# Six token blocks transposed beside the first attention, and four column tiles of their projection behind the first selection's products

## The chip, the cores and the metric

The kernel runs on one core of a Trainium2 chip. The metric is the device time of one execution in microseconds. The engines are named as the profile names them: PE does the matrix products and the transposes, PEld its weight loads, DVE is the vector engine, ACT the scalar engine, POOL the engine that also issues the indirect gathers, SP the queue that issues most other transfers. Each engine works through its own list of instructions in a fixed order.

## The reference

One decoder layer over 1024 tokens of width 1024, in float32:

```
x   = layer_norm(x)
mix = concat(fox_attention(x @ w_in), hgrn2(x @ w_in)) @ w_out
x   = layer_norm(alpha * x + mix)
q   = x @ w_q                            # 8 heads x 2 halves x 128
s   = q . sub_keys                       # 128 scores per half
top 16 of each half; top 16 of the 256 sums -> 128 experts e per token, gates g
h   = gelu(x . u_tab[e]) * g             # 128 numbers per token
y   = sum over e of h * v_tab[e]
out = layer_norm(alpha * x + y)
```

`fox_attention` has 8 causal heads of 64 with a forget bias, `hgrn2` 4 heads with a 128 x 128 state, worked through in chunks. There are 16,384 experts. Their part is computed in two ways: four of the eight blocks of 128 tokens fetch their experts' rows with gathers, the other four use a dense product with all experts, in which gates that were not chosen are zero.

## The kernel before

**Precision.** A float32 operand is split in a high and a low part (ACT copies to the high, DVE or POOL subtracts), and a product is three matrix products: high by high, low by high, high by low (`mm3`, L289 to L295). A weight block of 128 x 1024 so needs one load (`wraw`), one ACT copy (`whi`, L215) and one subtraction (`wlo`, L218). `transpose_split` (L267) turns a token block on PE and splits it out of PSUM (`xh` on ACT, `xl` on DVE at L286; with a third pool it goes by ACT's `tsx` copy at L283 and POOL at L284).

**Stages.** `mixers` (L323) takes the tokens as three groups of 256, 512 and 256. For each: the attention and the recurrence (`fox`, `hgrn`, interleaved), `mix_out` (the output projection, the residual, the norm, 16 transposes and their split `mh`, `ml`), `select` (scores, and DVE's top-16 searches) and `select_tail` (pair builds `oh`, `ij` on DVE, `sel`). The input projection is done twice: for the first group at the start, and for the later 768 tokens in one go behind the first group's `select_tail`. `preload` (L438) loads those six token blocks, `project` (L418) turns and splits them while the tail runs, and `project_cols` (L446) computes 17 column tiles (weights `wt`, 24 products 512 wide and 24 products 256 wide each) and then six groups of `wn` columns (144 products each).

**Side work.** The gathers and the one-hot matrices that the dense part needs are generators in three lists: `ujobs` (rows of `u`, one dot product each on DVE at L1124), `vjobs` (rows of `v`, accumulated on DVE at L1149 for three of the four blocks and on PE for one) and `bjobs` (the one-hots of the dense blocks, built on DVE at L962 and multiplied on PE). `tick` (L176) is called in every stage with the stage's name; it adds RATE times a weight to what is owed to each list, up to 16, and runs steps while something is owed. HOLD keeps the first list still for some ticks. What is left of the gathers runs in the dense part: `dense` (L1019) goes over 128 chunks of experts, products on PE, splits and sums (`dy`) on DVE, and a `tick` between. Gathered rows go through eight buffers named `rows`; `ys` is the accumulator of L1149, 128 x 1024 float32 in SBUF. `psy` is a PSUM pool with one tile `y` of two banks.

The order on each engine is set by the scheduler from the order of the code and the operations' priorities. The list above is the order of the code.

Of the kernel before, what the change touches and what calls it, by code (L numbers as in the profile page):

```python
# [8 lines left out]
F32 = mybir.dt.float32  # L9
F32R = mybir.dt.float32r  # L10
# [19 lines left out]
NROWS = 8  # L30
# [8 lines left out]
VDVE = (1, 6, 7)  # L39
HOLD = 7  # L40
# [7 lines left out]
GORD = (0, 1, 2, 3, 4, 5)  # L48
Q = {"qk": "a", "hs": "a"}
SEND0 = 0  # L50
# [22 lines left out]
class Layer:  # L73
    def __init__(self, ctx, tc, a, out, dbg=None):
        self.ctx, self.tc, self.nc, self.a, self.out = ctx, tc, tc.nc, a, out
        self.dbg = dbg
        self.nw, self.slabs = 0, 1
        self.ujobs, self.vjobs, self.bjobs, self.owed = [], [], [], [0.0] * 3
        self.nu = self.nv = 0
        self.hold = 0.0  # L80
# [94 lines left out]

    def tick(self, phase, T=None, w=1.0):  # L176
        rate = RATE[phase] if T is None else RATE[phase][T]
        self.hold = max(self.hold - w, 0.0)
# [144 lines left out]
    def mixers(self, groups, es):  # L323
        st, gb, tl = ExitStack(), ExitStack(), ExitStack()
        self.lx = ExitStack()
# [4 lines left out]
        for n, (t0, T) in enumerate(groups):  # L330
# [5 lines left out]
            if n < 2:  # L336
                tl.close()
            po = st.enter_context(self.pool("po", 1, "left"))
            whole = f"m{n}" in WHOLE
# [22 lines left out]
            pos = pz.tile([P, nq, 8, 16], U32, name="pos", tag="pos")  # L362
            if n == 0:
                x1 = self.preload(T, S - T)
            self.select(t0, T, mh, ml, sv, si, best, pos, T == 256 or EARLY)
# [9 lines left out]
            if n == 0:  # L375
                x1 = self.project(T, S - T, st, x1)
                self.lx.close()
            tail = self.select_tail(t0, T, sv, si, best, pos, T == 256 or EARLY, pw)
# [41 lines left out]
    def project(self, t0, T, st, xs=None):  # L420
        pa = st.enter_context(self.pool("pa", 1, "right"))
        xh = pa.tile([P, DC, T], F32R, name="xh", tag="xh")
        xl = pa.tile([P, DC, T], F32R, name="xl", tag="xl")

        def split(n, x):
            self.transpose_split("f", x, xh, xl, n)

        if t0:
            with self.pool("pt", 2, "right") as pt:
                for n, x in enumerate(xs):  # L430
                    self.transpose_split("f", x, xh, xl, n, pt if n % 2 < PSPL else None)
        else:
            pl = self.lx.enter_context(self.pool("pl", 2, "left"))
            self.first_ln(pl, 0, T, split)
            self.lns = [lambda r0=r0: self.first_ln(pl, r0, 2 * P, lambda n, x: None) for r0 in range(T, S, 2 * P)]
        return xh, xl

    def preload(self, t0, T):  # L438
        pl = self.lx.enter_context(self.pool("pl", 1, "left"))
        xs = []  # L440
        for n in range(T // P):
            x = pl.tile([P, D], F32, name="x", tag="x", bufs=T // P)
            self.q("x1l").dma_start(x, self.d_x1[t0 + n * P : t0 + (n + 1) * P])
            xs.append(x)
        return xs

    def project_cols(self, t0, T, xh, xl):
        nc, a = self.nc, self.a
        nq = T // P
        tsl = slice(t0, t0 + T)  # L450
        with self.pool("pb", 2, "right") as pb:
            for m in range(17):
                po = self.projT(self.weight(pb, a["wt"][m], "p1" if t0 else "p0"), xh, xl, T)
# [645 lines left out]

    def rows(self):  # L1100
        return self.gp.tile([P, D], F32, name="rows", tag="rows", bufs=NROWS)

# [26 lines left out]
    def gather_v(self, blk, u):  # L1129
# [6 lines left out]
        if blk in VDVE:  # L1136
            ys = gp.tile([P, D], F32, name="ys", tag="ys")
            ei = sel[:, 0].bitcast(I32)
# [178 lines left out]
```

## Time and profile before

| | |
|---|---|
| median of 3 runs | 3062.12 us (3060.14 to 3067.3) |
| the profiled execution | 3096.88 us, its span 3094.9 us |
| PE busy | 2628.0 us (85%), 15865 instructions |
| DVE busy | 2664.9 us (86%), 5563 instructions |
| POOL busy | 1614.0 us (52%), 1216 instructions |
| ACT busy | 1076.2 us (35%), 2004 instructions |
| HBM read, written | 821.67 MB, 62.42 MB |

The profiled execution stands 34.76 us above the median. In time the profile reads as follows: the first group's projection to about 121 us, its attention to 195, `mix_out` to 233, `select` to 298, `select_tail` to 352.5, the later tokens' projection to 584, the second group to about 1085, the third group's attention to 1343, its `mix_out` to 1366 and `select` with the rest of the one-hots to 1523, and the dense part from about 1595 to 3060. The row of PE's granted clock is between 0.7 and 0.9 up to the dense part and 0.9 and more in it.

### The profile page before, as it was taken

Reading aid. Unit: us, or ns where it says so; the run is one execution under the profiler, and the core shown is the slowest. Engines: PE = TensorE matmul, PEld = TensorE weight load, DVE = VectorE, ACT = ScalarE, POOL = GpSimd, SP = SyncE. Lnnn points to the kernel's source line nnn. Section 1 sums busy time; section 2 is a strip of 40 time slices with the busy share of each in tenths; the row PEclk is TensorE's granted clock in tenths of the full one; section 3 lists DMA queues with packets and bytes.
Section 4 is the critical chain, followed back from the end, with each engine's and each line's share of the span. In section 5 each row is a group of like instructions: output and inputs, shape, how many; then the busy total and the mean of one; then the engine's idle time right before and its main releaser. Section 6 shows DMA issues by size and latency. Waiting matters only on the chain. (4 is left out here: it accounts for less than half of the span.)

```text
span 3094.9 us, 45136 instructions
## 1 busy us (share of the span) xinstructions
PE 2628.0 (85%) x15865; PEld 2150.5 (69%) x15865; DVE 2664.9 (86%) x5563; ACT 1076.2 (35%) x2004; POOL 1614.0 (52%) x1216
## 2 busy tenths in 40 slices
PE   7767799777769767878469899999989999999995
PEld 6767689755557445667458778787768877877874
DVE  8658766588669986689888999999999999999998
ACT  4733222364222333476323223223223323222331
POOL 2344476565756644200045666665567665656652
PEclk9878899797889888889589999999999999999997
DMA  7542599754978856864479999999999999999994
GB/s 277 191 150 75 196 349 322 229 163 153 343 252 293 275 159 234 304 248 177 182 248 365 332 369 367 356 367 360 347 360 367 382 381 356 363 365 341 369 340 157
DMA packets 338659, 887.10 MB, mean 287 GB/s; under 512 B 29912, under 2 KB 124136, under 8 KB 336000
## 3 DMA queue, kind: packets, MB, share of 16 engines
q0 software_dynamic: 147456, 536.94, 47.5%
q1 hardware_dynamic: 185200, 338.38, 31.3%
q10 hardware_dynamic: 5776, 8.90, 0.8%
q8 instruction: 125, 2.05, 0.3%
q14 instruction: 102, 0.84, 0.1%
HBM read 821.67 MB, written 62.42 MB: 286 GB/s over the span
## 5 line engine op out<-in xcount | busy, mean ns | idle before, releaser
L1105 POOL DMA_INDIRECT rows<-in_u,gsel x512 | 687.4, 1343 | 617.8 <-DVE rows L1124 408.3
L1105 POOL DMA_INDIRECT rows<-in_v,gsel x512 | 642.8, 1256 | 444.5 <-DVE ys L1149 259.8
L1124 DVE SCALAR_TENSOR_TENSOR rows<-rows,gx 128x1024 f32<-128x1024 f32 x512 | 627.9, 1273 | 40.7 <-DMA rows<-in_u,gsel 20.5
L1149 DVE SCALAR_TENSOR_TENSOR ys<-rows,sd,ys 128x1024 f32<-128x1024 f32 x381 | 488.8, 1283 | 0.6
L293 PE MATMUL psh<-dxh,uh 128*128 128x512 f32 x1024 | 402.9, 393 | 29.4 <-ACT uh L1031 16.5
L295 PE MATMUL psh<-dxh,ul 128*128 128x512 f32 x1024 | 400.7, 391 | 9.5 <-DVE ul L1032 9.4
L294 PE MATMUL psh<-dxl,uh 128*128 128x512 f32 x1024 | 400.2, 391 | 0.0
L294 PE MATMUL psf<-vl,hh 128*128 128x512 f32 x768 | 309.9, 404 | 42.6 <-DVE vl L1032 41.8
L1031 ACT ACTIVATE vh<-vr 128x512 fp32r<-128x512 f32 x256 | 161.8, 632 | 429.2 <-PE psv L295 392.1
L295 PE MATMUL psf<-vh,hl 128*128 128x512 f32 x768 | 305.2, 397 | 0.0
L293 PE MATMUL psf<-vh,hh 128*128 128x512 f32 x768 | 278.8, 395 | 11.7 <-DVE dy L1064 8.1
L1031 ACT ACTIVATE uh<-ur 128x1024 fp32r<-128x1024 f32 x128 | 136.0, 1063 | 413.0 <-PE psh L294 386.2
L293 PEld LDWEIGHTS psh<-dxh,uh 128*128 128x128 f32 x1024 | 193.5, 189 | 77.2 <-ACT hs L1045 19.1
L295 PEld LDWEIGHTS psh<-dxh,ul 128*128 128x128 f32 x1024 | 193.5, 189 | 50.6 <-DVE ul L1032 10.5
L294 PEld LDWEIGHTS psh<-dxl,uh 128*128 128x128 f32 x1024 | 193.5, 189 | 39.5
L294 PEld LDWEIGHTS psf<-vl,hh 128*128 128x128 f32 x768 | 147.8, 192 | 89.6 <-DVE vl L1032 59.0
L215 ACT ACTIVATE whi<-wraw 128x1024 fp32r<-128x1024 f32 x106 | 111.5, 1056 | 231.5 <-issue 62.8
L1032 DVE TENSOR_TENSOR vl<-vr,vh 128x512 fp32r<-128x512 f32 x256 | 169.6, 683 | 13.9 <-ACT vh L1031 13.9
L293 PEld LDWEIGHTS psf<-vh,hh 128*128 128x128 f32 x768 | 145.1, 189 | 49.8 <-DVE dy L1064 9.6
L218 DVE TENSOR_TENSOR wlo<-wraw,whi 128x1024 fp32r<-128x1024 f32 x60 | 81.8, 1364 | 106.7 <-ACT whi L215 94.4
L295 PEld LDWEIGHTS psf<-vh,hl 128*128 128x128 f32 x768 | 147.9, 193 | 29.9
L1032 DVE TENSOR_TENSOR ul<-ur,uh 128x1024 fp32r<-128x1024 f32 x128 | 156.2, 1221 | 12.3 <-ACT uh L1031 11.2
(341 smaller groups left out, 6155.9 us busy)
## 6 DMA issues: line engine op xcount, KB each, us to landing
ur<-in_ut SPq DMA_DIRECT2D x128, 512.0 KB
vr<-in_v SPq DMA_DIRECT2D x256, 256.0 KB
d_g<-slab SPq DMA_DIRECT2D x16, 2048.0 KB
gt<-d_g SPq DMA_DIRECT2D x32, 1024.0 KB
wraw<-in_wq SPq DMA_DIRECT2D x48, 512.0 KB
wraw<-in_wt SPq DMA_DIRECT2D x34, 512.0 KB
wraw<-in_wn SPq DMA_DIRECT2D x24, 512.0 KB
wraw<-in_wo SPq DMA_DIRECT2D x24, 512.0 KB
```

What stands on the lines that cost most here:

```text
L215: nc.scalar.activation(hi, raw, AF.Copy)
L218: eng.tensor_tensor(lo, raw, hi.bitcast(F32), op=ALU.subtract)
L293: mm(out, lh, rh, start=start, stop=False, **kw)
L294: mm(out, lh, rl, start=False, stop=False, **kw)
L295: mm(out, ll, rh, start=False, stop=stop, **kw)
L1031: nc.scalar.activation(hi, raw, AF.Copy)
L1032: nc.vector.tensor_tensor(lo, raw, hi.bitcast(F32), op=ALU.subtract)
L1105: self.nc.gpsimd.indirect_dma_start(out=t, out_offset=None, in_=tab, in_offset=bass.IndirectOffsetOnAxis(ap=idx, axis=0))
L1124: self.pin(nc.vector.scalar_tensor_tensor(u, u, 1.0, x2, op0=ALU.mult, op1=ALU.mult, accum_out=sd[:, n : n + 1]), "u")
L1149: self.pin(nc.vector.scalar_tensor_tensor(ys, v, h, ys, op0=ALU.mult, op1=ALU.add), "w")
```

## The change

A generator `early` does what `preload` and `project` did for the six later token blocks, and the first four (NEARLY) of the 17 column tiles. `tick` advances it in the first group's attention (0.34 of a step for each tick there, some 18 ticks, so six steps) and returns without serving the three lists, or adding to what they are owed, while it lives (before, the first group's ticks left `bjobs` at its cap of 16 before it had a job; now it starts from nothing in the third group's attention); what is left, the four tiles, is emitted behind `select` and ahead of `select_tail`. The splits of the token blocks are on ACT and DVE, none on POOL; the four tiles' weights go through `rows` buffers, their low halves on DVE, their products into the PSUM tile `y`. HOLD goes from 7 to 3.5, and the accumulator at L1149 from SBUF to the PSUM tile `y`.

```
@@ -37,7 +37,7 @@
     "dense": (5.4, 5.4, 0),
 }
 VDVE = (1, 6, 7)
-HOLD = 7
+HOLD = 3.5
 LNM = (3, 6, 9)
 QB, PRB = {256: 2, 512: 2}, {2: 3, 4: 7}
 VRAW = 5
@@ -46,6 +46,8 @@
 FAST = {"x": 2, 0: 2, 256: 2, 768: 2}
 FLN = 9
 GORD = (0, 1, 2, 3, 4, 5)
+NEARLY = 4
+ERATE = {"fox": 0.34, "hgrn": 0.0, "mix": 0.0, "sel": 0.0}
 Q = {"qk": "a", "hs": "a"}
 SEND0 = 0
 WDIV = {"p0": 0, "m0": 1, "s0": 1, "p1": 3, "m1": 2, "s1": 2, "m2": 1, "s2": 1}
@@ -76,6 +78,7 @@
         self.dbg = dbg
         self.nw, self.slabs = 0, 1
         self.ujobs, self.vjobs, self.bjobs, self.owed = [], [], [], [0.0] * 3
+        self.ahead, self.due = None, 0.0
         self.nu = self.nv = 0
         self.hold = 0.0
         self.lnf = None
@@ -174,6 +177,12 @@
         yield
 
     def tick(self, phase, T=None, w=1.0):
+        if self.ahead and phase in ERATE:
+            self.due += w * ERATE[phase]
+            while self.due >= 1.0:
+                self.due -= 1.0
+                next(self.ahead, None)
+            return
         rate = RATE[phase] if T is None else RATE[phase][T]
         self.hold = max(self.hold - w, 0.0)
         for n, q in enumerate((self.ujobs, self.vjobs, self.bjobs)):
@@ -321,7 +330,7 @@
         return po
 
     def mixers(self, groups, es):
-        st, gb, tl = ExitStack(), ExitStack(), ExitStack()
+        st, gb, tl, ex = ExitStack(), ExitStack(), ExitStack(), ExitStack()
         self.lx = ExitStack()
         init = self.setup()
         next(init)
@@ -335,6 +344,11 @@
             st.close()
             if n < 2:
                 tl.close()
+            ex.close()
+            if n == 0:
+                pa = ex.enter_context(self.pool("pa", 1, "right"))
+                x1 = [pa.tile([P, DC, S - T], F32R, name=m, tag=m) for m in ("xh", "xl")]
+                self.ahead = self.early(T, S - T, *x1, pa)
             po = st.enter_context(self.pool("po", 1, "left"))
             whole = f"m{n}" in WHOLE
             mh = po.tile([P, DC, T], F32 if whole else F32R, name="mh", tag="mh")
@@ -360,8 +374,6 @@
             si = pz.tile([P, nq, 16, 16], U32, name="si", tag="si")
             best = pz.tile([P, nq, 8, 16], F32, name="best", tag="best")
             pos = pz.tile([P, nq, 8, 16], U32, name="pos", tag="pos")
-            if n == 0:
-                x1 = self.preload(T, S - T)
             self.select(t0, T, mh, ml, sv, si, best, pos, T == 256 or EARLY)
             if late:
                 self.drain(self.bjobs)
@@ -373,8 +385,8 @@
                 dense = self.dense_prep(es)
             pw = tl.enter_context(self.pool("pw", 1, "right"))
             if n == 0:
-                x1 = self.project(T, S - T, st, x1)
-                self.lx.close()
+                self.drain([self.ahead])
+                self.ahead = None
             tail = self.select_tail(t0, T, sv, si, best, pos, T == 256 or EARLY, pw)
             if T == 256:
                 tail = self.tail_gather(t0, T, tail)
@@ -425,31 +437,49 @@
         def split(n, x):
             self.transpose_split("f", x, xh, xl, n)
 
-        if t0:
-            with self.pool("pt", 2, "right") as pt:
-                for n, x in enumerate(xs):
-                    self.transpose_split("f", x, xh, xl, n, pt if n % 2 < PSPL else None)
-        else:
-            pl = self.lx.enter_context(self.pool("pl", 2, "left"))
-            self.first_ln(pl, 0, T, split)
-            self.lns = [lambda r0=r0: self.first_ln(pl, r0, 2 * P, lambda n, x: None) for r0 in range(T, S, 2 * P)]
+        pl = self.lx.enter_context(self.pool("pl", 2, "left"))
+        self.first_ln(pl, 0, T, split)
+        self.lns = [lambda r0=r0: self.first_ln(pl, r0, 2 * P, lambda n, x: None) for r0 in range(T, S, 2 * P)]
         return xh, xl
 
-    def preload(self, t0, T):
-        pl = self.lx.enter_context(self.pool("pl", 1, "left"))
-        xs = []
+    def early(self, t0, T, xh, xl, pa):
+        nc, a = self.nc, self.a
         for n in range(T // P):
-            x = pl.tile([P, D], F32, name="x", tag="x", bufs=T // P)
+            x = self.rows()
             self.q("x1l").dma_start(x, self.d_x1[t0 + n * P : t0 + (n + 1) * P])
-            xs.append(x)
-        return xs
+            pt = self.psy.tile([P, D], F32, name="y", tag="y")
+            for c in range(DC):
+                nc.tensor.transpose(pt[:, c * P : (c + 1) * P], x[:, c * P : (c + 1) * P], self.ident)
+            sl = slice(n * P, (n + 1) * P)
+            for c0 in range(0, DC, 4):
+                v = pt[:, c0 * P : (c0 + 4) * P].rearrange("p (c t) -> p c t", c=4)
+                h = xh[:, c0 : c0 + 4, sl]
+                nc.scalar.activation(h, v, AF.Copy)
+                nc.vector.tensor_tensor(xl[:, c0 : c0 + 4, sl], v, h.bitcast(F32), op=ALU.subtract)
+            yield
+        for m in range(NEARLY):
+            raw, hi, lo = self.rows(), self.rows(F32R), self.rows(F32R)
+            self.q("w").dma_start(raw, a["wt"][m])
+            nc.scalar.activation(hi, raw, AF.Copy)
+            nc.vector.tensor_tensor(lo, raw, hi.bitcast(F32), op=ALU.subtract)
+            wh, wl = (t.rearrange("p (c m) -> p c m", c=DC) for t in (hi, lo))
+            po = self.psy.tile([P, D], F32, name="y", tag="y")
+            s = pa.tile([P, T], F32, name="es", tag="es", bufs=2)
+            for c0 in range(0, T, 512):
+                cs = slice(c0, min(c0 + 512, T))
+                for dc in range(DC):
+                    self.mm3(po[:, cs], wh[:, dc], wl[:, dc], xh[:, dc, cs], xl[:, dc, cs], dc == 0, dc == DC - 1)
+                nc.scalar.activation(s[:, cs], po[:, cs], AF.Copy, scale=0.125 if m < 4 else 1.0)
+            h = m % 4
+            self.q("qk").dma_start((self.d_q, self.d_k)[m // 4][h * P : (h + 1) * P, t0 : t0 + T], s)
+            yield
 
     def project_cols(self, t0, T, xh, xl):
         nc, a = self.nc, self.a
         nq = T // P
         tsl = slice(t0, t0 + T)
         with self.pool("pb", 2, "right") as pb:
-            for m in range(17):
+            for m in range(NEARLY if t0 else 0, 17):
                 po = self.projT(self.weight(pb, a["wt"][m], "p1" if t0 else "p0"), xh, xl, T)
                 self.tick("proj", T)
                 if m in LNM and self.lns:
@@ -1097,8 +1127,8 @@
                     prev = down(g, h)
             self.finish_dense(dv[0], y, dv[1])
 
-    def rows(self):
-        return self.gp.tile([P, D], F32, name="rows", tag="rows", bufs=NROWS)
+    def rows(self, dt=F32):
+        return self.gp.tile([P, D], dt, name="rows", tag="rows", bufs=NROWS)
 
     def gather_rows(self, tab, idx):
         t = self.rows()
@@ -1134,7 +1164,7 @@
         nc.scalar.activation(sd, sd, AF.Gelu)
         nc.vector.tensor_tensor(sd, sd, gt, op=ALU.mult)
         if blk in VDVE:
-            ys = gp.tile([P, D], F32, name="ys", tag="ys")
+            ys = self.psy.tile([P, D], F32, name="y", tag="y")
             ei = sel[:, 0].bitcast(I32)
             vs = []
             for k in range(P + LAG):
```

On PE, at the end of the first group's `mix_out` and the start of `select`, before (`psf<-whi,ml` is the output projection, `psf<-ident,res` the transposes behind the norm, `psf<-mh,whi` the first products of `select`):

```order
1003 L295 MATMUL psf<-whi,ml 128x256
1004 L294 MATMUL psf<-wlo,mh 128x256
1005 L295 MATMUL psf<-whi,ml 128x256
1006 L275 MATMUL psf<-ident,res 128x128 x16
1007 L293 MATMUL psf<-mh,whi 128x256
1008 L294 MATMUL psf<-ml,whi 128x256
```

and now, where `y<-xh,rows` is a product of an early column tile:

```order
1066 L304 MATMUL psf<-whi,ml 128x256
1067 L304 MATMUL y<-xh,rows 128x512
1068 L302 MATMUL y<-xh,rows 128x512
1069 L303 MATMUL y<-xl,rows 128x512
1108 L284 MATMUL psf<-ident,res 128x128 x8
1111 L284 MATMUL psf<-ident,res 128x128 x4
1112 L302 MATMUL y<-xh,rows 128x256
1115 L284 MATMUL psf<-ident,res 128x128 x4
1116 L302 MATMUL y<-xh,rows 128x512
```

41 products of the second tile stand ahead of the transposes and five among them; 24 products 512 wide and 14 products 256 wide of the third tile stand behind them and ahead of the first product of `select`. The first tile stands likewise ahead of the output projection, 16 of its 48 products ahead of the attention's last two transposes and 32 behind them.

On PE at the end of `select`, where `psf<-kt,qt` are the scores, before:

```order
1404 L295 MATMUL psf<-mh,wlo 128x256
1405 L837 MATMUL psf<-kt,qt 128x128 x4
1406 L275 MATMUL psf<-ident,x 128x128 x48
1407 L293 MATMUL psf<-xh,whi 128x512
1408 L294 MATMUL psf<-xl,whi 128x512
```

and now:

```order
1557 L304 MATMUL psf<-mh,wlo 128x256
1558 L867 MATMUL psf<-kt,qt 128x128 x2
1559 L304 MATMUL y<-xh,rows 128x256
1560 L867 MATMUL psf<-kt,qt 128x128 x2
1561 L302 MATMUL y<-xh,rows 128x256
1564 L302 MATMUL y<-xh,rows 128x512
```

The 48 transposes are gone from this place, and the fourth tile stands there in their stead. The projection proper begins behind it with its fifth tile. Up to the second (last) transpose of the tail's indices, `psh<-ident,eo`, 62 products 512 wide of the projection stood in the list before, and 28 now.

On DVE in the third group's attention, where `oh`, `ij` are pair builds of the second group's tail and `nm` is the maximum that a row of the attention waits for, before:

```order
1756 L895 TENSOR_TENSOR oh<-oh,fi 128x2048
1757 L593 TENSOR_REDUCE dg<-md 128x128
1758 L897 TENSOR_TENSOR oh<-oh 128x1024
1759 L613 SCALAR_TENSOR_TENSOR state<-state,eb,psh 128x128
1760 L897 TENSOR_TENSOR oh<-oh 128x512
1761 L686 TENSOR_REDUCE nm<-psf 128x1
```

and the same maximum now:

```order
1684 L591 TENSOR_TENSOR E<-b 128x128x2
1685 L766 TENSOR_TENSOR o<-o,rsy 128x256
1686 L592 TENSOR_TENSOR E<-b 128x128x2
1687 L596 TENSOR_TENSOR X<-k,E 128x128x2
1688 L716 TENSOR_REDUCE nm<-psf 128x1
```

Between this maximum and the one before it stand 52 rows before, with two pair builds, and 24 now, with the end of one. One-hots have moved back with it: of the 232 of the kernel, 214 stood ahead of the last pair build of the third group's selection before, and 190 do now.

## Rows read from the trace of the kernel before

**Rows 1.** Windows by stage: busy us and (instructions) of each engine, granted clock, transfers.
```profile
core 0: us, PE busy (x) PEld busy (x) DVE busy (x) ACT busy (x) POOL busy (x), PEclk, DMA share, GB/s
121.00:195.00 74.00, 45.24 (x606) 36.76 (x604) 53.10 (x148) 37.25 (x105) 30.24 (x30) 0.68 0.47 157
220.00:233.00 13.00, 3.71 (x17) 3.17 (x16) 10.18 (x24) 3.48 (x5) 0.00 (x0) 0.61 0.28 106
233.00:298.00 65.00, 58.67 (x450) 57.93 (x451) 56.28 (x317) 23.22 (x44) 31.17 (x13) 0.92 0.27 85
298.00:352.50 54.50, 26.94 (x111) 20.20 (x109) 53.44 (x176) 14.98 (x27) 12.12 (x8) 0.72 0.21 70
352.50:480.50 128.00, 127.98 (x757) 114.15 (x758) 73.37 (x117) 31.61 (x48) 91.03 (x64) 1.00 0.94 345
1366.00:1523.00 157.00, 123.11 (x995) 105.02 (x993) 151.41 (x571) 89.94 (x222) 0.00 (x0) 0.85 0.47 182
1595.00:3060.00 1465.00, 1393.50 (x5989) 1126.75 (x5987) 1420.66 (x1904) 427.10 (x629) 916.12 (x678) 0.99 0.97 356
```

**Rows 2.** PE's timeline, end of the first attention: start, us, instruction, idle before.
```profile
195.28 0.69 PE L741 MATMUL psf<-ident,o 128*128 128x128 f32 x2 [6.26 <-DVE o L736]
```

**Rows 3.** PE's timeline, norm of the first group.
```profile
228.39 3.65 PE L275 MATMUL psf<-ident,res 128*128 128x128 f32 x16 [8.33 <-DVE res L262]
```

**Rows 4.** DVE's timeline, its first search in the first selection.
```profile
241.30 0.49 DVE L807 MAX8 sv<-s 128x8 f32<-128x128 f32 x2 [6.98 <-ACT s L840]
```

**Rows 5.** DVE's timeline in the first selection's tail.
```profile
316.42 1.29 DVE L885 CAST plo<-psh 128x128 f32<-128x128 uint32 x1
317.74 1.18 DVE L886 TENSOR_SCALAR psh<-pos 128x128 uint32<-128x128 uint32 x1
318.96 1.18 DVE L887 CAST ptm<-psh 128x128 f32<-128x128 uint32 x1
320.07 1.28 DVE L286 TENSOR_TENSOR xl<-psf,xh 128x512 fp32r<-128x512 f32 x2
...
327.07 0.23 DVE L885 CAST plo<-psh 128x128 f32<-128x128 uint32 x1
```

**Rows 6.** POOL's timeline in the same tail.
```profile
315.29 4.77 POOL L284 TENSOR_TENSOR xl<-tsx,xh 128x512 fp32r<-128x512 f32 x3 [28.49 <-ACT tsx L283]
...
332.01 2.57 POOL L218 TENSOR_TENSOR wlo<-wraw,whi 128x1024 fp32r<-128x1024 f32 x1 [3.27 <-ACT whi L215]
```

**Rows 7.** PE's timeline, inside the later tokens' projection.
```profile
399.72 0.39 PE L293 MATMUL psf<-xh,whi 128*128 128x512 f32 x1
...
402.44 0.28 PE L293 MATMUL psh<-xh,whi 128*128 128x256 f32 x1
...
403.99 0.28 PE L294 MATMUL psh<-xl,whi 128*128 128x256 f32 x1
```

**Rows 8.** PE's timeline in the third group's attention.
```profile
1116.91 1.14 PE L715 MATMUL psf<-ident,pr 128*128 128x128 f32 x4 [16.83 <-ACT pr L693]
```

**Rows 9.** DVE's timeline, one-hots near the end of the third selection.
```profile
1511.04 0.68 DVE L962 TENSOR_TENSOR ohi<-iota16h,gpair 128x1024 f16<-128x1024 f16 x1
1511.65 0.68 DVE L962 TENSOR_TENSOR ohj<-iota16h,gpair 128x1024 f16<-128x1024 f16 x1
```

**Rows 10.** DVE's groups by form: count, busy us, mean ns, idle before, releaser.
```profile
L1124 DVE SCALAR_TENSOR_TENSOR rows<-rows,gx 128x1024 f32<-128x1024 f32 x512 | 627.9, 1273 | 40.7 <-DMA rows<-in_u,gsel 20.5 <-issue 9.5 <-DMA gx<-d_x 8.8
L1149 DVE SCALAR_TENSOR_TENSOR ys<-rows,sd,ys 128x1024 f32<-128x1024 f32 x381 | 488.8, 1283 | 0.6
L1032 DVE TENSOR_TENSOR vl<-vr,vh 128x512 fp32r<-128x512 f32 x256 | 169.6, 683 | 13.9 <-ACT vh L1031 13.9
L1064 DVE TENSOR_TENSOR dy<-dy,psf 128x512 f32<-128x512 f32 x192 | 125.5, 676 | 1.9 <-PE psf L295 1.9
...
L1228 DVE SCALAR_TENSOR_TENSOR rows<-rows,ys 128x1024 f32<-128x1024 f32 x3 | 3.6, 1216 | 0.0
```

**Rows 11.** The accumulator's operations: ns least, median and most.
```profile
L1149 DVE SCALAR_TENSOR_TENSOR ys<-rows,sd,ys x381: 1265/1276/3818, 1968.9 to 3055.2; 128x1024 f32<-128x1024 f32 x191
```

More of the change, by code (lines that the diff above doesn't have):

```diff
@@ L78, in __init__ @@
         self.ujobs, self.vjobs, self.bjobs, self.owed = [], [], [], [0.0] * 3
+        self.ahead, self.due = None, 0.0
         self.nu = self.nv = 0
@@ L176, in tick @@
     def tick(self, phase, T=None, w=1.0):
+        if self.ahead and phase in ERATE:
+            self.due += w * ERATE[phase]
+            while self.due >= 1.0:
+                self.due -= 1.0
+                next(self.ahead, None)
+            return
         rate = RATE[phase] if T is None else RATE[phase][T]
@@ L337, in mixers @@
                 tl.close()
+            ex.close()
+            if n == 0:
+                pa = ex.enter_context(self.pool("pa", 1, "right"))
+                x1 = [pa.tile([P, DC, S - T], F32R, name=m, tag=m) for m in ("xh", "xl")]
+                self.ahead = self.early(T, S - T, *x1, pa)
             po = st.enter_context(self.pool("po", 1, "left"))
@@ L426, in split @@
             self.transpose_split("f", x, xh, xl, n)
[L428 to L435, printed above, removed]
+        pl = self.lx.enter_context(self.pool("pl", 2, "left"))
@@ L436, in project, with early @@
+        self.first_ln(pl, 0, T, split)
+        self.lns = [lambda r0=r0: self.first_ln(pl, r0, 2 * P, lambda n, x: None) for r0 in range(T, S, 2 * P)]
         return xh, xl
-    def preload(self, t0, T):
-        pl = self.lx.enter_context(self.pool("pl", 1, "left"))
-        xs = []
+    def early(self, t0, T, xh, xl, pa):
+        nc, a = self.nc, self.a
         for n in range(T // P):
-            x = pl.tile([P, D], F32, name="x", tag="x", bufs=T // P)
+            x = self.rows()
             self.q("x1l").dma_start(x, self.d_x1[t0 + n * P : t0 + (n + 1) * P])
-            xs.append(x)
-        return xs
+            pt = self.psy.tile([P, D], F32, name="y", tag="y")
+            for c in range(DC):
+                nc.tensor.transpose(pt[:, c * P : (c + 1) * P], x[:, c * P : (c + 1) * P], self.ident)
+            sl = slice(n * P, (n + 1) * P)
+            for c0 in range(0, DC, 4):
+                v = pt[:, c0 * P : (c0 + 4) * P].rearrange("p (c t) -> p c t", c=4)
+                h = xh[:, c0 : c0 + 4, sl]
+                nc.scalar.activation(h, v, AF.Copy)
+                nc.vector.tensor_tensor(xl[:, c0 : c0 + 4, sl], v, h.bitcast(F32), op=ALU.subtract)
+            yield
+        for m in range(NEARLY):
+            raw, hi, lo = self.rows(), self.rows(F32R), self.rows(F32R)
+            self.q("w").dma_start(raw, a["wt"][m])
+            nc.scalar.activation(hi, raw, AF.Copy)
+            nc.vector.tensor_tensor(lo, raw, hi.bitcast(F32), op=ALU.subtract)
+            wh, wl = (t.rearrange("p (c m) -> p c m", c=DC) for t in (hi, lo))
+            po = self.psy.tile([P, D], F32, name="y", tag="y")
+            s = pa.tile([P, T], F32, name="es", tag="es", bufs=2)
+            for c0 in range(0, T, 512):
+                cs = slice(c0, min(c0 + 512, T))
+                for dc in range(DC):
+                    self.mm3(po[:, cs], wh[:, dc], wl[:, dc], xh[:, dc, cs], xl[:, dc, cs], dc == 0, dc == DC - 1)
+                nc.scalar.activation(s[:, cs], po[:, cs], AF.Copy, scale=0.125 if m < 4 else 1.0)
+            h = m % 4
+            self.q("qk").dma_start((self.d_q, self.d_k)[m // 4][h * P : (h + 1) * P, t0 : t0 + T], s)
+            yield
@@ L451, in project_cols @@
         with self.pool("pb", 2, "right") as pb:
-            for m in range(17):
+            for m in range(NEARLY if t0 else 0, 17):
                 po = self.projT(self.weight(pb, a["wt"][m], "p1" if t0 else "p0"), xh, xl, T)
@@ L1098, in dense, with rows @@
             self.finish_dense(dv[0], y, dv[1])
-    def rows(self):
-        return self.gp.tile([P, D], F32, name="rows", tag="rows", bufs=NROWS)
+    def rows(self, dt=F32):
+        return self.gp.tile([P, D], dt, name="rows", tag="rows", bufs=NROWS)
     def gather_rows(self, tab, idx):
@@ L1136, in gather_v @@
         if blk in VDVE:
-            ys = gp.tile([P, D], F32, name="ys", tag="ys")
+            ys = self.psy.tile([P, D], F32, name="y", tag="y")
             ei = sel[:, 0].bitcast(I32)
```

12 lines of the change are left out of this document (6 added, 6 removed).

## The prediction

> **What bounds the kernel now.** I read the windows by stage first, then the timelines of PE and DVE at the places where the change puts or removes work, then DVE's groups by form. The profiled execution took 3096.88 us, 34.8 us more than the median of 3062.12; the sum is made against the profile, and its difference is then taken off the median.
>
> The windows [rows 1] show a different limit in each stage. In the first attention (121 to 195) nothing is full: PE works 45.24 of 74 us and DVE 53.10; it is a chain between engines. In the norm (220 to 233) PE works 3.71 of 13 us and waits. In the selection (233 to 298) DVE works 56.28 of 65 us: its first search starts at 241.30 after 6.98 us of idling for scores [rows 4], and from there it is full. In the tail (298 to 352.5) DVE works 53.44 of 54.5 us, PE only half the time. [...] The third selection is DVE again (151.41 of 157). In the dense part DVE works 1420.66 of 1465 us, PE 1393.50, and the transfers take 0.97 of the DMA engines: three limits within a few per cent.
>
> So the reader is to see a hole of PE's between 195 and 352.5, in a stretch that DVE limits, followed by a stretch that PE limits. Work moved from the second into the first is worth its full time if PE's order in the hole doesn't make DVE late, because a DVE that is full from 241 to 352 gives back no delay.
>
> **The change part by part.** A product 512 wide is issued every 0.227 us (12 from 399.72 to 402.44) and one 256 wide every 0.12 us (13 from 402.44 to 403.99) [rows 7]. A column tile is 24 of each: 5.4 + 2.9 = 8.3 us. Four are 33.2 us.
>
> 1. *First attention.* Six blocks bring DVE 12 subtractions of 512 columns at 0.6 us (two in a row took 1.28 us [rows 5]), and the weights three of twice that width, so some 1.2 each: 10.8 us in a stage with 20.9 us of idle DVE. ACT gets 12 high halves and the same weights, PE 48 transposes. On SP the four early weight loads wait for `rows` buffers and stand ahead of the output projection's loads. What hides this is the stage's slack; if it sat wholly on the chain it would cost 10.8. In return mix_out's weights are prepared later, which takes up to one POOL half of 2.57 us [rows 6] off the chain. I take +3, with ends -3 and +11.
>
> 2. *First tile ahead of the output projection.* 16 of its 48 products (3.6 us) fall in PE's idle 6.26 us before the transposes of `o` [rows 2]; 8 wide and 24 narrow ones, 1.8 + 2.9 = 4.7 us, stand behind these and ahead of the output projection. Its first weight's high half now stands on ACT behind the tile's copy. Ends: 0 if the whole tile fits into the 6.26 us, 8 if the weight's low half (2.57 on POOL [rows 6]) comes late as well. I take +4.5.
>
> 3. *Second and third tile at the norm.* 46 products of the second (24 wide, 22 narrow: 8.1 us) have PE's idle 8.33 us before the transposes [rows 3]. 38 of the third, 24 x 0.227 + 14 x 0.12 = 7.1 us, stand ahead of the selection's first product, where PE had about 1 us free (13 - 3.71 - 8.33 [rows 1, 3]). That delays DVE's first search by some 6 us, and DVE carries this to the end of the tail. If the granted clock stays at 0.61 there, the second tile overruns its gap and it is +13; if the busier PE raises it, the 16 transposes (3.65 us [rows 3]) run faster and +4 is left. I take +6.
>
> 4. *Tail.* Six subtractions leave DVE: 3.6 us. Beside POOL's three subtractions of 4.77 us [rows 6], three small DVE operations took 3.65 us from 316.42 to 320.07, of which one took 0.23 alone [rows 5]: some 3.2 us of waiting for POOL leave too. Together -7; ends -10 (the other three POOL subtractions delay DVE as much) and -3.6 (POOL's weight halves take their place).
>
> 5. *Projection.* PE has four tiles less: -33.2. But 62 of its wide products stood ahead of the tail's last transpose, 14.1 us of work done in the tail; now 28 do, 6.4 us. Net -25.5, I take -25. Ends: -27, and -12 if the transfers take over (rival 3).
>
> 6. *One-hots.* `bjobs` starts the third attention with nothing owed, so a burst of pair builds before one row maximum shrinks. There PE waited 16.83 us [rows 8]. The work isn't gone: 24 more one-hots stand behind the third selection's last pair build, at 0.605 us [rows 9] 14.5 us, on a DVE that is full there [rows 1]. I take 0, with ends -17 (the gap closes, the end is covered) and +14.5.
>
> 7. *Gathers.* Four dot products of `ujobs` fall out of the projection and are done in the dense part: 4 x 1.273 = 5.1 us on DVE [rows 10]. +5, with 0 as the other end, if PE or the transfers cover it.
>
> 8. *Accumulator in PSUM.* 381 operations of 1283 ns [rows 10], no one of which wrote PSUM before. Operations that read one operand from PSUM don't cost more: `dy<-dy,psf` takes 676 ns, `vl<-vr,vh` 683, both 512 wide [rows 10]. Mean over median is 7 ns [rows 10, 11], 2.7 us in all, from single operations of up to 3818 ns beside another engine's use of SBUF, which one SBUF operand less may avoid. Two operations of the same size, `ys` and `L1228`, differ by 67 ns for operand forms alone [rows 10]; a step of that size for PSUM would be 381 x 0.067 = 25.5. I take -0.5, the nearest row being `dy`; ends -3 and +25.
>
> [...]
>
> Sum: 3 + 4.5 + 6 - 7 - 25 + 0 + 5 - 0.5 = -14. The profile would be 3083 us, the median 3048.
>
> **The rivals.**
>
> *1. PE's early products eat the gain.* Terms 1 to 3 at their upper ends are 32 instead of 13.5: the sum becomes +4.5 at most; halfway there it is -5. For it: the order puts 78 early products directly ahead of work that DVE waits for, and DVE has no slack behind. Against it: PE's two waits of 6.26 and 8.33 us hold most of a tile each. Time: 3057 to 3067, most of it within 0.2% (6.1 us, about what a measurement of this kernel can tell) of before.
>
> *2. The accumulator in PSUM is dear.* The place is the dense part and its gathers, where DVE is the fullest engine; the price is per operation. At 67 ns it costs 25 and the sum is +11: 3073, slower. From 37 ns on (14 us over 381) the gain is gone. Against it is the `dy` row, which reads PSUM; for it, that no row writes there and reads back the same bank at once.
>
> *3. The transfers bind the projection.* They take 0.94 of the DMA engines there [rows 1]. Four tiles need 2 MB of weights less and four gather steps 2 MB less, of 44 MB (345 GB/s x 128 us): 9%, or 12 us of 128. Then term 5 is -12 and the sum -1: 3061. Against it: PE waits for nothing in these 128 us, and the gathers are paced by tiles and go with them.
>
> *4. The burst goes for good.* Term 6 at -17: sum -31, time 3031. For it is the wait of 16.83 us [rows 8]; against it the full DVE behind. Its opposite, +14.5 with a gap that only moves, gives 0: 3062.
>
> **How the numbers follow.** Forecast (terms near their values, 3038 to 3056): 0.46. Rival 1: 0.16. Rival 2 and other costs of the accumulator: 0.10. Rival 3: 0.06. Rival 4: 0.13, its opposite 0.09. Faster by over 0.2%: the forecast, rival 4 and a quarter of rival 1, 0.63. Within 0.2%: the rest of rival 1 up to its end, rival 3 and half of the opposite, 0.21. Slower: rival 2, the other half and what adds up on top of rival 1, 0.16. The range, 3024 to 3070, takes in rival 4 and cuts off rival 2 at its full price.
>
> **What would show it.** Four tiles of `y<-` products between the last `psv` and 298; the first search of the first selection 10 to 15 us later than 241; no POOL work in the tail and its small DVE operations back at 0.2 us; the projection's end some 18 us earlier. The mean of the operations into `y` at the accumulator's line: about 1276 ns if right, 1340 if rival 2 holds. PE's wait of 16.83 us gone or shorter, and one-hots that end later behind the last pair build. The prediction is wrong at its root if the first search comes over 25 us late, or if the projection doesn't shorten by some 25 us.

## The result, and the profile after

The changed kernel is slower: a median of 3091.05 us (5 runs, 3085.96 to 3099.76) against 3067.30 (5 runs) before, a ratio of 1.0079 with a 95% interval of 1.0064 to 1.0094. A later set gave 1.0088 (1.0068 to 1.0109). 3048 was forecast, with a range of 3024 to 3070; 3091 lies outside it.

The two first traces don't show this: the profiled executions took 3096.88 and 3093.22 us. So the kernel before was profiled once more (first experiment below: 3070.6 us). The 26 us that its first trace has more come from the third attention: from its first product to the transposes behind its norm it took 308.2 us there and 278.3 in the second, and the gathered rows that PE sums in it ended at 1312.8 and 1284.6 us. Everything up to there agrees within 2 us. From here on "before" is this second trace.

Ahead of the dense part the change did what was forecast, and more. The rows are windows by stage with the columns of [rows 1]; first the kernel before, from the first search to the end of the tail and then the projection:

```profile
241.70:353.00 111.30, 77.75 (x498) 70.53 (x496) 108.45 (x488) 34.89 (x65) 40.28 (x20) 0.82 0.24 82
353.00:584.60 231.60, 231.58 (x1619) 217.65 (x1619) 140.65 (x211) 58.26 (x80) 170.41 (x114) 1.00 0.91 327
```

The same two stretches of the changed kernel:

```profile
255.10:351.50 96.40, 69.27 (x463) 63.32 (x462) 94.70 (x481) 25.88 (x49) 31.10 (x13) 0.88 0.26 89
351.50:558.40 206.90, 206.89 (x1461) 193.77 (x1461) 140.78 (x200) 51.18 (x69) 160.97 (x109) 0.99 0.93 341
```

The first search comes 13.4 us later, the selection with its tail is 14.9 us shorter, the projection 24.7 us: at its end the changed kernel is 26.2 us ahead. It begins the dense part 22.5 us ahead, and ends the whole 22.8 us behind. All of the loss is in the dense part. Its window from the first product `psh<-dxh,uh` to the last, before:

```profile
1512.00:3009.40 1497.40, 1411.24 (x6047) 1141.98 (x6048) 1438.90 (x1949) 434.51 (x637) 924.45 (x685) 0.97 0.96 353
```

and in the changed kernel:

```profile
1489.50:3032.00 1542.50, 1432.15 (x6048) 1152.87 (x6049) 1444.72 (x1958) 435.19 (x637) 891.54 (x691) 0.96 0.95 344
```

It is 45.1 us longer, with only 5.8 us more of work on DVE (5.1 of it the four dot products) and the same number of products on PE. DVE idles 97.8 us in it instead of 58.5. Who waits for whom is in the groups by form of this window (count, busy us, mean ns, idle before, releaser). Before:

```profile
L293 PE MATMUL psf<-vh,hh 128*128 128x512 f32 x744 | 269.9, 395 | 6.8 <-DVE dy L1064 3.4 <-ACT vh L1031 3.1
L293 PE MATMUL psv<-vh,hh 128*128 128x512 f32 x248 | 97.2, 392 | 0.3 <-DVE dy L1064 0.3
L1149 DVE SCALAR_TENSOR_TENSOR ys<-rows,sd,ys 128x1024 f32<-128x1024 f32 x369 | 474.6, 1286 | 0.6
L1032 DVE TENSOR_TENSOR ul<-ur,uh 128x1024 fp32r<-128x1024 f32 x128 | 156.6, 1223 | 13.7 <-ACT uh L1031 13.0
```

and after, the answers to [rows 10] among them:

```profile
L302 PE MATMUL psf<-vh,hh 128*128 128x512 f32 x744 | 275.6, 403 | 33.3 <-DVE dy L1094 32.0 <-ACT vh L1061 1.0
L302 PE MATMUL psv<-vh,hh 128*128 128x512 f32 x248 | 99.2, 400 | 14.2 <-DVE dy L1094 14.2
L1179 DVE SCALAR_TENSOR_TENSOR y<-rows,sd,y 128x1024 f32<-128x1024 f32 x370 | 476.0, 1286 | 1.8 <-DMA rows<-in_v,gsel 1.7
L1062 DVE TENSOR_TENSOR ul<-ur,uh 128x1024 fp32r<-128x1024 f32 x128 | 156.4, 1224 | 37.5 <-ACT uh L1061 37.5
```

The accumulator's operations are not dearer: 1286 ns in SBUF, 1286 in PSUM. What grew are waits in a circle: PE waits for `dy` (which frees the `psf` or `psv` tile that the next product needs) 46.2 us instead of 3.7, and DVE waits for ACT's `uh` 37.5 us instead of 13.0, which ACT makes when PE has used the last one.

### The profile page after: what moved, and what is told of

Read it like the earlier page. It is cut to its first block, busy times and chain, and to the rows that moved or that the text cites. A ratio compares the mean times of both kernels' runs of the same rounds, so it can differ in the third digit from the quotient of the medians.

```text
span 3091.4 us, 45093 instructions
## 1 busy us (share of the span) xinstructions
PE 2634.0 (85%) x15865; PEld 2144.1 (69%) x15865; DVE 2668.0 (86%) x5570; ACT 1071.1 (35%) x1997; POOL 1563.7 (51%) x1209
## 4 chain that ended last, share of the span: by engine, by line
PE 27%; DVE 14%; issue 6%; DMA 2%; ACT 1%; POOL 1%; SPq 0%; DVEq 0%; POOLq 0%; ACTq 0%
DVE rows L1154 5%; DVE y L1179 4%; PE psh L304 4%; PE psh L302 4%; PE psh L303 4%; PE psf L303 4%; PE psf L304 4%; PE psf L302 3%; PE psv L303 1%; DVE dy L1094 1%; PE psv L304 1%; DVE vl L1062 1%; POOL rows L1135 1%; PE psv L302 1%; DMA rows<-in_u,gsel 1%
## 5 line engine op out<-in xcount | busy, mean ns | idle before, releaser
L1135 POOL DMA_INDIRECT rows<-in_u,gsel x512 | 699.2, 1366 | 593.2 <-DVE rows L1154 377.1
L1135 POOL DMA_INDIRECT rows<-in_v,gsel x512 | 592.6, 1157 | 523.3 <-DVE y L1179 356.4
L1154 DVE SCALAR_TENSOR_TENSOR rows<-rows,gx 128x1024 f32<-128x1024 f32 x512 | 638.1, 1288 | 56.1 <-DMA rows<-in_u,gsel 54.5
L1179 DVE SCALAR_TENSOR_TENSOR y<-rows,sd,y 128x1024 f32<-128x1024 f32 x381 | 490.1, 1286 | 1.9 <-DMA rows<-in_v,gsel 1.7
L303 PE MATMUL psf<-vl,hh 128*128 128x512 f32 x768 | 316.7, 412 | 34.0 <-DVE vl L1062 31.4
L302 PE MATMUL psf<-vh,hh 128*128 128x512 f32 x768 | 285.3, 403 | 38.8 <-DVE dy L1094 37.6
L302 PEld LDWEIGHTS psh<-dxh,uh 128*128 128x128 f32 x1024 | 193.4, 189 | 72.2 <-ACT uh L1061 16.3
L303 PEld LDWEIGHTS psh<-dxl,uh 128*128 128x128 f32 x1024 | 193.4, 189 | 39.3
L1062 DVE TENSOR_TENSOR ul<-ur,uh 128x1024 fp32r<-128x1024 f32 x128 | 156.4, 1224 | 37.5 <-ACT uh L1061 37.5
L227 POOL TENSOR_TENSOR wlo<-wraw,whi 128x1024 fp32r<-128x1024 f32 x45 | 109.9, 2446 | 122.7 <-ACT whi L224 122.5
```

The lines of the kernel that those rows point to most:

```text
L227: eng.tensor_tensor(lo, raw, hi.bitcast(F32), op=ALU.subtract)
L302: mm(out, lh, rh, start=start, stop=False, **kw)
L303: mm(out, lh, rl, start=False, stop=False, **kw)
L1062: nc.vector.tensor_tensor(lo, raw, hi.bitcast(F32), op=ALU.subtract)
L1135: self.nc.gpsimd.indirect_dma_start(out=t, out_offset=None, in_=tab, in_offset=bass.IndirectOffsetOnAxis(ap=idx, axis=0))
L1154: self.pin(nc.vector.scalar_tensor_tensor(u, u, 1.0, x2, op0=ALU.mult, op1=ALU.mult, accum_out=sd[:, n : n + 1]), "u")
```

## The experiments

Theory A: the accumulator in PSUM lengthens the dense part. Its rival: the dense part is longer because of what comes before it. When A had held, it was split in A1 (the order that the scheduler makes with a PSUM accumulator) and A2 (PSUM itself). Each set of runs had its own runs of the kernel before on the same chip, and ratios are to those; the second set ("Order or PSUM" and "How many steps") had a before of 3105.96 us, and the one trace of it in before's order has 316 us in the third attention where the first set has 278. So times and ratios of that set are not put beside those of the others; lengths of the dense part are. The dense lengths below run, as above, from the first to the last `psh<-dxh,uh`.

**The kernel before again.** No edit.

> The kernel before, unchanged, profiled a second time. Its first profile (3096.88 us) stood 34.8 us above its median, the changed kernel's (3093.22) only 2 us above its own, so the two traces can't be subtracted as they are. Theory A (the first profile was one of a slow execution of the same program): the ratio is 1.000, this profile's time is 3060 to 3075, and the 20 to 35 us less show in the dense part (1541 to 3034 before). Rival B (profiling itself costs the kernel before 30 us): this profile's time is again 3090 to 3100.

3067.2 us, ratio 0.9999 (0.9988 to 1.0010); the profiled execution took 3070.6, its span 3068.6. The excess of the first profile is no cost of profiling. But it lies in the third attention, not in the dense part (1497.4 us here, 1492.6 there): this expectation had the place wrong.

**The accumulator alone.**

```diff
-            ys = gp.tile([P, D], F32, name="ys", tag="ys")
+            ys = self.psy.tile([P, D], F32, name="y", tag="y")
```

> The kernel before with the accumulator of the gathered v rows in PSUM, nothing else changed. The dense part of the changed kernel took 48 us longer than before's (1542 against 1493 us) though it does the same products. Theory A (the accumulator in PSUM lengthens the dense part, by its place in the scheduler's order or by its operations): 20 to 45 us slower than before. Rival B (the dense part is longer because of what comes before it: steps owed, an earlier start): within 8 us of before, accumulator operations at 1283 to 1286 ns.

3101.87 us, ratio 1.0107 (1.0092 to 1.0122): 33 us for one line. Its dense part:

```profile
1508.40:3041.00 1532.60, 1428.49 (x6047) 1153.24 (x6048) 1439.53 (x1950) 434.65 (x637) 875.37 (x686) 0.96 0.95 345
```

35.2 us longer than before's, with DVE's work the same to 0.7 us.

**The changed kernel without it** (`self.dx` is the pool of the dense part's sums, kept under that name in another line).

```diff
-            ys = self.psy.tile([P, D], F32, name="y", tag="y")
+            ys = self.dx.tile([P, D], F32, name="ys", tag="ys")
```

> The changed kernel with the accumulator of the gathered v rows back in SBUF, in the pool of the dense part's sums. Theory A (the accumulator in PSUM lengthens the dense part): 20 to 45 us faster than the changed kernel, so 3045 to 3070, at or below before. Rival B: within 8 us of the changed kernel, 3085 to 3098.

3065.74 us, ratio 0.9994 (0.9982 to 1.0005). A holds for some 25 us. But this kernel begins the dense part 18.9 us ahead of before and ends level:

```profile
1493.10:3007.20 1514.10, 1421.81 (x6047) 1147.70 (x6048) 1443.20 (x1957) 434.63 (x637) 947.03 (x689) 0.97 0.96 350
```

16.7 us longer, of which the four moved dot products are 4.3 of DVE's work.

**What is owed to the one-hots**, kept as before.

```diff
                 next(self.ahead, None)
+            r = RATE[phase] if T is None else RATE[phase][T]
+            self.owed[2] = min(self.owed[2] + w * r[2], 16.0)
             return
```

> The changed kernel, but ticks of the first group go on adding to what is owed to the one-hots' list, as before, so that it starts the third attention with 16 owed: 212 instead of 188 one-hots ahead of the last search of the third selection. Theory A (the loss lies in the dense part): the dense part begins up to 35 us later than in the changed kernel (1489) and the whole is 0 to 30 us slower, 3091 to 3120. Rival C (starting with nothing owed costs time in the end): up to 25 us faster than the changed kernel.

3089.05 us, ratio 1.0065 (1.0047 to 1.0083), hardly apart from the changed kernel. From the third attention's first product to the transposes behind its norm it takes 277.7 us, as before (278.3), and the changed kernel 261.6; but its dense part begins at 1488.5, the changed kernel's at 1489.5. Rival C falls, and so does the later start that A expected: 14 of the 16 us come back between that norm and the dense part. The order of the dense part is the changed kernel's, instruction by instruction, and it takes 1538.4 us.

**Order or PSUM.** Here every engine's instructions are tied by order edges (no waits) to the sequence that another build has (the loop alone is shown; the lists of names are left out):

```diff
+    for p, q in zip(names, names[1:]):          # one list for each engine
+        tc.add_manual_dep(made[q], p, mybir.DependencyInfo(
+            mybir.DependencyClass.NoSync, mybir.DependencyReason.DATA), reason="order")
```

First the kernel before with its accumulator in PSUM, in the order of the kernel before:

> The kernel before with the accumulator in PSUM, as in the run b_psum (33 us slower than before, its operations no longer than before's), but every engine's instructions held by added order edges in exactly the order that they have in the kernel before; only the place of the accumulator differs from before. Theory A1 (the loss is the order that the scheduler makes when the accumulator is in PSUM): within 6 us of before, 3060 to 3075. Rival A2 (the loss is in PSUM itself: the operations, or PE's and ACT's access to PSUM beside them): as slow as b_psum, 3092 to 3105.

Ratio 1.0002 (0.9984 to 1.0021), 3105.54 us beside 3105.96. The dense part:

```profile
1547.80:3045.30 1497.50, 1414.76 (x6048) 1144.54 (x6049) 1436.68 (x1949) 434.24 (x637) 893.50 (x685) 0.97 0.96 353
```

0.1 us from before's. A1 holds by the ratio and A2 falls: PSUM itself costs nothing that the ratio can tell. Between the two builds with a PSUM accumulator only the order differs: from the dense part's first product to the end, 611 of the 1717 vector instructions and 1733 of the 6146 products stand at another place. Why the scheduler orders them otherwise when this tile lies in PSUM, no run shows.

Then the changed kernel in the order that it has with an SBUF accumulator:

> The changed kernel, accumulator in PSUM, with every engine held in the order that the same kernel has with its accumulator in SBUF (the run a_sbuf, 3066). Theory A1 (order): 3060 to 3073, no slower than before. Rival A2 (PSUM itself): 3085 to 3098, as the changed kernel.

Ratio 0.9950 (0.9931 to 0.9969), 3088.42 us; dense part 1515.6 us, as in the run with SBUF (1514.1), and 27 us under the changed kernel's. By this length A1 holds. The time alone would fall in A2's range, but before was 38 us slower in this set; and the ratio is lower than that of the run with SBUF (0.9994) mostly because the third attention lengthened less in this order (286 against 259 us) than in before's (316 against 278).

**What that order does** is to be seen at one place, near 2260 us of the run with the accumulator alone (start, us, instruction, idle before). DVE, ACT and PE:

```profile
2256.16 1.27 DVE L1064 TENSOR_TENSOR dy<-dy,psf 128x512 f32<-128x512 f32 x2
...
2257.96 1.21 DVE L1124 SCALAR_TENSOR_TENSOR rows<-rows,gx 128x1024 f32<-128x1024 f32 x1
...
2263.69 0.68 DVE L1064 TENSOR_TENSOR dy<-dy,psf 128x512 f32<-128x512 f32 x1
2264.29 0.68 DVE L1064 TENSOR_TENSOR dy<-dy,psv 128x512 f32<-128x512 f32 x1
...
2264.42 0.80 PE L293 MATMUL psf<-vh,hh 128*128 128x512 f32 x1 [6.43 <-DVE dy L1064]
...
2269.49 0.63 ACT L1031 ACTIVATE vh<-vr 128x512 fp32r<-128x512 f32 x1 [12.53 <-PE psv L295]
...
2270.15 0.69 DVE L1032 TENSOR_TENSOR vl<-vr,vh 128x512 fp32r<-128x512 f32 x1 [1.71 <-ACT vh L1031]
2273.28 0.69 DVE L1032 TENSOR_TENSOR vl<-vr,vh 128x512 fp32r<-128x512 f32 x1 [2.44 <-ACT vh L1031]
2278.42 1.23 DVE L1032 TENSOR_TENSOR ul<-ur,uh 128x1024 fp32r<-128x1024 f32 x1 [4.45 <-ACT uh L1031]
```

Five dot products (2257.96 to 2263.69) stand between the second and the third of the four `dy`. PE waits 6.43 us for the third; ACT's next `vh` waits for PE; and then DVE, the fullest engine, waits three times, 8.6 us in all. In the order of the kernel before (the run with the PSUM accumulator tied to it) the four sums of this place stand together:

```profile
2293.64 1.23 DVE L1124 SCALAR_TENSOR_TENSOR rows<-rows,gx 128x1024 f32<-128x1024 f32 x1 [1.44 <-DMA rows<-in_u,gsel]
2294.79 0.08 DVE L1124 DVE_READ_ACCUMULATOR rows<-rows,gx 128x1 f32 x1
2294.79 1.88 DVE L1064 TENSOR_TENSOR dy<-dy,psf 128x512 f32<-128x512 f32 x3
2296.59 0.68 DVE L1064 TENSOR_TENSOR dy<-dy,psv 128x512 f32<-128x512 f32 x1
```

**How many steps are left to the dense part.** With the SBUF accumulator, `NEARLY = 0` (212 dot products ahead of the dense part instead of 196), and separately `HOLD = 0` (208):

> The changed kernel with its accumulator in SBUF and no early column tile (NEARLY 0): the six blocks are still turned beside the first attention. 212 dot products of the gathers instead of 196 stand ahead of the dense part. By the prediction's steps 2, 3 and 5 the first search of the first selection comes some 10 us earlier than in a_sbuf (255.2) and the projection ends some 14 us later than there (558.6). Theory D (what is won ahead of the dense part reaches the end): the whole is 3060 to 3075 with a dense part shorter by up to 20 us for the 16 steps fewer in it, and longer ahead by 14. Rival E (the tiles are worth their full time): 3078 to 3090.

> The changed kernel with its accumulator in SBUF and HOLD 0 in place of 3.5: 208 instead of 196 dot products ahead of the dense part. a_sbuf begins the dense part 19 us earlier than before and ends with it, since its dense part is 17 us longer (1514 against 1497 us). Theory D (the dense part is longer for the steps moved into it, about 1.28 us and its transfers each): the dense part is 10 to 16 us shorter than in a_sbuf, the projection up to 6 us longer, the whole 3050 to 3062, faster than both. Rival F (the dense part's length doesn't follow the number of steps): 3062 to 3072.

Ratios 1.0067 (1.0043 to 1.0091) and 1.0009 (0.9990 to 1.0029), times 3123.44 and 3109.95 us in the set whose before took 3105.96; dense parts 1514.1 and 1517.5 us. With 16 and 12 steps fewer the dense part is no shorter than with 196 (1514.1). Theory D falls; the ratios, on a before of 3067, are at 3088 and 3070 us, as rivals E and F have it. Each of the two has an order of its own in the dense part; that the order counts and not the number, the next runs show. Without the tiles the first search starts at 252.4 us, 3 earlier than with them and not 10, and the projection ends 32 us later, not 14.

**The order of the kernel before by itself.** With `HOLD = 3` there are 200 dot products ahead of the dense part, as before, and with the accumulator in SBUF the scheduler then makes the dense order of the kernel before, instruction by instruction. This set has the changed kernel in it as well:

> The changed kernel as it is, as the reference for the three others on the same chip. Theory A1 (the scheduler's order of the dense part): its dense part takes 1542 us again and the ratio to before is 1.006 to 1.010, or somewhat less where the third attention is slower, as in the runs psum_in_b_order and a_in_sbuf_order.

> The changed kernel with its accumulator in SBUF and HOLD 3 in place of 3.5. 200 dot products then stand ahead of the dense part, as in the kernel before, and every engine's order in the dense part is, instruction by instruction, that of the kernel before. Theory A1: the dense part takes 1497 us, what is won ahead of it (19 to 23 us) reaches the end, the ratio is 0.991 to 0.995 and faster than the changed kernel by 1.3 to 1.6%. Rival G (the dense part's end is set by something else, so an earlier start is lost): ratio 0.998 to 1.002, as a_sbuf.

> The changed kernel, accumulator in PSUM as changed, HOLD 3, and the dense part held by added order edges in the order that it has in the kernel before. Theory A1: the same as a_sbuf_h3 within 5 us, dense part 1497 us. Rival A2 (PSUM itself costs time in the dense part): 20 us or more above a_sbuf_h3.

The changed kernel: 1.0088, dense part 1545.1 us. `HOLD = 3` with SBUF: 3053.76 us, ratio 0.9957 (0.9940 to 0.9973). `HOLD = 3` with PSUM, dense part tied to before's order: 3047.16 us, ratio 0.9943 (0.9923 to 0.9963). Their dense parts:

```profile
1497.80:2991.10 1493.30, 1413.34 (x6047) 1142.85 (x6048) 1438.58 (x1949) 434.49 (x637) 929.45 (x685) 0.98 0.97 354
```

```profile
1493.90:2983.80 1489.90, 1412.82 (x6048) 1142.88 (x6049) 1436.95 (x1949) 433.90 (x637) 884.92 (x685) 0.98 0.97 355
```

Both beat both kernels. A1 held again. The SBUF ratio is just outside its expected 0.991 to 0.995, since the dense part begins 14.2 us ahead of before's and not 19 to 23; and the run with PSUM is 6.6 us faster, a little beyond the 5 expected and the opposite of A2. In all, the six traces in before's order, two of them with PSUM, have dense parts of 1489.9 to 1502.8 us; no trace in another order is under 1514.1.

**The tiles alone**: the same with `NEARLY = 0`, `HOLD = 7`.

> The changed kernel with its accumulator in SBUF, no early column tile (NEARLY 0) and HOLD 7: the six blocks are still turned beside the first attention, 200 dot products stand ahead of the dense part and its order is that of the kernel before. Against a_sbuf_h3 it shows the worth of the four tiles alone, against before that of the early transposes and of starting with nothing owed. By the prediction's steps the four tiles are worth 25 less the 10.5 that they delay, 14.5 us, and the transposes some 4 to 10 us less 3: ratio 0.997 to 1.000, and 10 to 18 us slower than a_sbuf_h3. Rival E (the tiles' delay ahead of the selection eats their worth): within 5 us of a_sbuf_h3.

3081.77 us, ratio 1.0051 (1.0033 to 1.0068), 28.0 us behind `HOLD = 3` with the tiles: more than the 10 to 18 expected, and rival E falls. It is also slower than before, where 0.997 to 1.000 was expected: without the tiles the rest of the change loses time. The projection ends 5.9 us later than before's, the dense part begins 10.3 us later, and in before's order it takes 1502.8 us.

With the tiles the projection ends at 557.9 instead of 590.5 us, so there they are worth 32.6 of their 33.2 us; at the start of the dense part 24.5 are left (1497.8 and 1522.3). They hardly delay the selection: without them the first search starts at 252.5, with them at 254.6, before at 241.7. From the first transpose behind the norm to that search it is 12.9 us before, 23.7 without the tiles and 23.2 in the changed kernel. What delays it is seen in the changed kernel:

```profile
235.36 1.41 SPq L223 DMA_DIRECT2D wraw<-in_wq  x3
...
243.62 1.06 ACT L224 ACTIVATE whi<-wraw 128x1024 fp32r<-128x1024 f32 x1 [0.34 <-DMA wraw<-in_wq]
...
255.13 0.49 DVE L837 MAX8 sv<-s 128x8 f32<-128x128 f32 x2 [17.85 <-ACT s L870]
```

and in the run without tiles:

```profile
238.89 1.06 ACT L224 ACTIVATE whi<-wraw 128x1024 fp32r<-128x1024 f32 x1 [5.12 <-DMA wraw<-in_wq]
...
240.00 0.58 PE L302 MATMUL psf<-mh,whi 128*128 128x256 f32 x1 [7.56 <-ACT whi L224]
```

The selection's first weights are issued at 235.36 and 232.14 us, and in the kernel before at 176.19, in the first attention:

```profile
176.19 1.60 SPq L214 DMA_DIRECT2D wraw<-in_wq  x3
```

Why they come later I have not tried; with the change, `pa` (48 KB of each partition) is held from the first attention on, where the weights' pool may have had its place. The tiles come nearly free because PE waits for these weights in any case; what they would cost with the weights loaded as early as before, no run shows.

## Why the prediction was wrong

Step by step, against the second trace of before:

| step | forecast | measured |
|---|---|---|
| 1, first attention | +3 | -2.2 (`psf<-ident,o` 195.6 to 193.4) |
| 2, first tile | +4.5 | +5.5 (from the transposes of `o` to the output projection: 0.3 to 5.9) |
| 3, to the first search | +6 | +10.1 (what is left of 13.4) |
| 4, selection and tail | -7 | -14.9 |
| 5, projection | -25 | -24.7 |
| 6, one-hots | 0 | the gain at the projection's end, 26.2, is 22.5 at the dense part's start |
| 7 and 8, dense part | +4.5 | +45.1 |

The failed step is 8, "Accumulator in PSUM": I took -0.5 from the duration of one operation, and rival 2 priced its +25 by duration too; a new order of the dense part has no term in the sum. The duration was right: 1286 ns in both places, where 1 ns less was forecast. What I didn't ask is what the scheduler does with a tile in another memory: it made another order of the dense part, and in a stretch where DVE, PE and the transfers are at 94 to 96% that order cost 28 (1542.5 against 1514.1) to 35 us (1532.6 against 1497.4). Rival 2 so had the right edit and size by the wrong mechanism: it can't be seen in the operation's mean, the row I had named for it. Neither of the two signs of a wrong root came, and none that I had named looks at the length of the dense part. A price of PSUM shows neither in a read (in the changed kernel `dy<-dy,psf`, with one operand there, took 682 ns and `vl<-vr,vh`, with none, 689) nor in the accumulation, which reads and writes PSUM (1286 ns in either place).

Step 7 failed in kind. Four steps more cost what they should (4.3 us of DVE's work), but with their number the order changed as well, and that is by all signs the larger part of the 16.7 us: with 200 instead of 196 they are gone (1493.3). No run has 196 steps in before's order, so the split between work and order is argued.

Step 3 was short by 4 us and had the wrong cause: I counted PE's early products and missed that the selection's weights were no longer loaded ahead. The products fill PE's wait for them. By its own terms the step would have been +4, for PE's clock did rise there (1.00 from 223.6 to 245.1 us, against 0.61 in [rows 1]) and the 16 transposes took 2.70 us instead of 3.65. That steps 1 to 3 add up to 13.4 us, where 13.5 was forecast, is luck. I had listed the loads that the change adds to SP's queue, not those that it takes from ahead. Step 4 was mis-sized: beside the subtractions that it counted, two weight halves left DVE there (2.3 us), and the other operations are 6.3 us shorter in sum, where 3.2 of waiting for POOL were counted. One long operation beside a weight half of POOL stayed: an `oh` of 2.47 us before (0.42 alone), a `psh<-pos` of 2.38 now (0.21 alone).

Step 6 was right, for the reason given: with the 16 kept as owed the dense part begins 1.0 us earlier. Rivals 1 and 3 did not come: the tiles gave 33 us and PE had no wait in the projection. Without the order's cost (and with `HOLD = 3`) the kernel runs in 3047 us, where 3048 was forecast; for the change as it stands that is no excuse, since the order is part of it, and the agreement is luck: the gain of that run is 20 us on a before of 3067.26, not 14 on 3062.12.

## What to carry to other kernels

Where a scheduler sets the order, an edit far from the bottleneck (a tile's memory, a count of steps) can reorder it, and in a stretch with several full engines that alone moved the time by 1% here (28 to 35 us): compare the order there, not only the operations. Tying one build to another's order by edges splits "the operation is slower" from "the order is worse" in one run. And when work is moved early, look for the loads that used to run ahead there: here the selection's first weights were issued at 235.36 us instead of 176.19.

## What the hardware showed that was not expected

The operation over 128 x 1024 that adds a scaled row to the accumulator took 1287 ns at the median in PSUM and 1279 in SBUF, while the first one of a block, which only scales, took 1281 instead of 743 ns. Before (ns least, median and most), and in the run with PSUM in before's order:

```profile
L1149 DVE SCALAR_TENSOR_TENSOR ys<-rows,sd,ys x381: 1265/1279/3811, 1940.3 to 3029.2; 128x1024 f32<-128x1024 f32 x191
L1147 DVE TENSOR_SCALAR ys<-rows,sd x3: 742/743/754, 1930.4 to 2757.9; 128x1024 f32<-128x1024 f32 x3
```

```profile
L1149 DVE SCALAR_TENSOR_TENSOR y<-rows,sd,y x381: 1270/1287/1302, 1976.1 to 3064.9; 128x1024 f32<-128x1024 f32 x191
L1147 DVE TENSOR_SCALAR y<-rows,sd x3: 1278/1281/1287, 1965.6 to 2797.1; 128x1024 f32<-128x1024 f32 x3
```

Why the scaling is slower in PSUM, no run shows. The one operation of 3.8 us [rows 11], at 2800.17, ran beside POOL's `rows<-rows,dlb` (L266, 2.41 us from 2800.49); in the changed kernel the two accumulations beside that operation of POOL (2.41 us from 2782.44) took 1285 and 1286 ns in PSUM, and none there or in the run shown here took over 1302. And the same order of instructions took 278 us in the third attention in the first set of runs, 316 us in the second and 308 us in the first trace of before; the gathered rows that PE sums there ended at 1284.6, 1319.7 and 1312.8 us. No run here shows why.
